# A hybrid decoder block on one core: ScalarE alone reads the turned banks of q and k, and the zero column of a weight tile is set by the engine that takes its differences

## The chip, the core and the metric

The kernel runs on one core of a Trainium2 chip. A core has TensorE (PE; its weight loads are listed apart as PEld), VectorE (DVE), ScalarE (ACT), GpSimd (POOL) and SyncE (SP), which issues transfers. Each engine takes its own instructions in the order in which they were written to its queue, and waits for the others through semaphores. The metric is the device time of one execution in microseconds (us), the median over runs; lower is better.

## The reference, cut to what matters

One decoder layer over 1024 tokens of width 1024, all in float32: a projection of the normalized input into three groups of heads (a short convolution, attention, a gated MLP), an output projection, a squared-ReLU MLP of width 4096 and a gated embedding. The change lies in the attention group, and there in two places: the normalized q and k, and the step from `log_rem` to `weights`.

```
q = rms_norm(q.reshape(bsz, s_len, 8, 64), q_norm_g)
k = rms_norm(k.reshape(bsz, s_len, 8, 64), k_norm_g)
...
z = einsum('bqhd,bkhd->bhqk', q, k) * 64 ** -0.5        # blocks of 128 queries
causal = s_pos < t_pos
log_beta = log_sigmoid(z)
log_rem = where(causal, log_sigmoid(-z), 0.0)
suffix = cumsum(log_rem, axis=3, reverse=True) - log_rem
weights = where(causal, exp(log_beta + suffix), 0.0)
o = einsum('bhqk,bkhd->bqhd', weights, v)
```

## The kernel before, in words

A float32 operand of a product is kept as two tiles, a `hi` part in the type fp32r and a `lo` part, the rest (`src - hi`). A product is then three matmuls, hi by hi, hi by lo and lo by hi (`product`, L157; `run`, L808). ScalarE makes the hi parts and VectorE, mostly, the lo parts (`split`, L131).

The program has four stages by the profile's clock: a first one to about 85 us (gating MLP, first projection), attention to about 395 us, the rest of the convolution and the output projection, and from about 480 us on the MLP and the gate. The change lies in the first two.

`project(pr)` (L345) makes q, k and v for a pair of heads. For each of eight blocks of 128 tokens, 24 matmuls write `qkv_ps`; the mean square of each head goes ScalarE (`qk_sq`, L376), VectorE (`ss`, L379), GpSimd (`rs`, L170), and VectorE scales q and k with it into the tile `qk` (L384). ScalarE and VectorE then write the two parts of `V` (L391).

Two blocks later, so to speak, `turn_qk` (L395) handles a pair of blocks: TensorE transposes four 128x128 squares of `qk` into one PSUM bank, `qk_tr`, q on its left half and k on its right. ScalarE writes the hi part of q (`QS`, L137 through `split`), VectorE its lo part (`q_lo`, L138), ScalarE the hi part of k (`KH`, L407), and VectorE its lo part in two halves of 64 partitions (`KL`, L409). All five read the bank. After the last block of a half (t = 3 and 7), six copies (L413 to L418) rearrange the parts. `qk_tr` comes from the pool `ps_tr` of three banks, in which the attention's own transposes `w_tr` take their turn too.

`attend(pr)` (L423) works on the same pair of heads. `stick(hh, g)` makes two rows of 128 queries (t = 2g and 2g+1) of head hh: matmuls `z` (L448, L450), a sigmoid on ScalarE into `rem` (L452), a scan on VectorE (L457; its backward running product is the exponential of the suffix sums), and the differences of neighbours into the weight tile `wt` (L464), on VectorE for t = 3, 5, 7 and on GpSimd for the others. The last column of `wt` is set to zero by GpSimd before that (L463). `wt` has four buffers. `gather(hh, g)` transposes the weight tiles into `w_tr` (L486), splits them (`wT_hi` on ScalarE, `wT_lo` on VectorE) and multiplies with `V` (`av`, L504). Head 0 goes through g = 0 to 3, head 1 through g = 3 to 0, so the wide rows of head 1 follow on those of head 0.

While pair `pr` is attended to, the projection of the next pair (for the last pair, the convolution) is woven in as fill for TensorE (`weave`, L269). The order in which the code is emitted isn't the order on the engines: the program is scheduled as a whole (`schedule_with_timeline_sim`, L1341), so that a changed instruction can move its neighbours on all engines.

Of the kernel before, what the change touches and what calls it, by code (L numbers as in the profile page):

```python
# [10 lines left out]
AF = mybir.ActivationFunctionType  # L11
ALU = mybir.AluOpType
# [21 lines left out]
def hybrid_block(ctx: ExitStack, tc: tile.TileContext, a: dict):  # L34
# [5 lines left out]
    nc = tc.nc  # L40
# [84 lines left out]
    gq = load_const("gq", [P, 1])  # L125
# [5 lines left out]
    def split(src, hi, lo, scale=None, low=nc.vector):  # L131

        if scale is None:
            last_hi[0] = nc.scalar.copy(hi, src)  # L134
            low.tensor_tensor(out=lo, in0=src, in1=hi, op=ALU.subtract)  # L135
        else:
            nc.scalar.activation(hi, src, AF.Copy, scale=scale)  # L137
            nc.vector.scalar_tensor_tensor(out=lo, in0=src, scalar=scale, in1=hi,  # L138
                                           op0=ALU.mult, op1=ALU.subtract)
# [255 lines left out]
    def turn_qk(head, t, qk):  # L395

        QS, KH, KL, _, low_q = head
        th = t // 4
        tr = bank(ps_tr, "qk_tr")
        for i in range(2):  # L400
            for j in range(2):
                o = j * 256 + i * P
                nc.tensor.transpose(tr[:, o:o + P], qk[:, i, j * P:(j + 1) * P], ident)
        ws = slice((t % 4 - 1) * P, (t % 4 + 1) * P)

        split(tr[:, :256], QS[0][th][:, ws], low_q[th][:, ws], scale=gq)
        nc.scalar.activation(KH[0][th][:, ws], tr[:, 256:], AF.Copy, scale=gk)  # L407
        for hh, own in enumerate((lo_p, hi_p)):
            nc.vector.scalar_tensor_tensor(out=KL[hh][th][own, ws], in0=tr[own, 256:],  # L409
                                           scalar=gk[own], in1=KH[0][th][own, ws],  # L410
                                           op0=ALU.mult, op1=ALU.subtract)
        if t % 4 == 3:
            nc.scalar.copy(KH[1][th][hi_p], KH[0][th][hi_p])  # L413
            nc.scalar.copy(KH[1][th][lo_p], KH[0][th][hi_p])
            nc.scalar.copy(KH[0][th][hi_p], KH[0][th][lo_p])
            nc.vector.tensor_copy(QS[1][th][hi_p], QS[0][th][hi_p])
            nc.vector.tensor_copy(QS[1][th][lo_p], low_q[th][hi_p])
            nc.vector.tensor_copy(QS[0][th][hi_p], low_q[th][lo_p])  # L418
        return 8
# [3 lines left out]
    def attend(pr):  # L423

        QS, KH, KL, V, _ = heads[pr]
# [11 lines left out]
        def stick(hh, g):  # L437
            weights[hh, g] = []
            for t in (2 * g, 2 * g + 1):
                W = (t + 1) * P  # L440
                th, ts = block(t)
                rem = at.tile([P, T], F32, tag="rem", name=name("rem"), bufs=3)
                wt = at.tile([P, T], F32, tag="wt", name=name("wt"), bufs=4)
                for kh in reversed(range(th + 1)):
                    n = min(HT, W - kh * HT)
                    ks = slice(kh * HT, kh * HT + n)
                    z = bank(ps_z, "z")[:, :n]
                    nc.tensor.matmul(z, QS[hh][th][:, ts], KH[hh][kh][:, :n],  # L448
                                     start=True, stop=False)
                    nc.tensor.matmul(z, QS[hh][th][:, ts], KL[hh][kh][:, :n],  # L450
                                     start=False, stop=True)
                    last_act[0] = nc.scalar.activation(rem[:, ks], z, AF.Sigmoid,  # L452
                                                       scale=-HD ** -0.5)


                back = rem[:, :W][:, ::-1]
                nc.vector.tensor_tensor_scan(out=back, data0=back,  # L457
                                             data1=after[:, T - W:][:, ::-1], initial=1.0,
                                             op0=ALU.mult, op1=ALU.max)


                on_vector = t in (3, 5, 7)
                nc.gpsimd.memset(wt[:, W - 1:W], 0.0)  # L463
                done = (nc.vector if on_vector else nc.gpsimd).tensor_tensor(  # L464
                    out=wt[:, :W - 1], in0=rem[:, 1:W], in1=rem[:, :W - 1], op=ALU.subtract)
                if not on_vector:
                    last_pool[0] = done
                weights[hh, g].append(wt)
                yield 2 * (t + 1) + 8
# [455 lines left out]
    for h in range(2):  # L925
        for n in (0, 4, 1, 5, 2, 6, 3, 7):
# [28 lines left out]
            t = hg[n][h] = late_slot("tmp", "hg")  # L955
# [29 lines left out]
    for i in range(FT):  # L985
# [19 lines left out]
        if i == 0:  # L1005
# [6 lines left out]
            for p, bank in last_k:  # L1012
                done = run(bank, up_pairs.pop((0, p)), hn[p], False, True, slice(3, 4))
# [27 lines left out]
        done = product_up(bc, 4, False, True)  # L1041
# [98 lines left out]
    for s, (c, p, j) in enumerate(steps):  # L1140
# [13 lines left out]
        elif p == 6:  # L1154
            subtract(nc.vector, u_sum[j], u_sum[j], bank)
            if last:
                add(nc.vector, h_res[j][1], h_res[j][1], u_sum[j])
                for h in range(2):
                    t = residual(j + 4, h)
                    subtract(nc.vector, t, t, u_sum[j])  # L1160
        elif p in (2, 3):
            t = residual(j, p - 2)
# [3 lines left out]
        else:  # L1166
            h = 0 if p == 4 else 1
            t = residual(j + 4, h)
# [55 lines left out]
    for p in GATE:  # L1224
        for j in range(4):
# [14 lines left out]
            for bank, c in zip(banks, cs):  # L1240
                done = run(bank, w, [cols(b, c) for b in h3[p]], p not in MATE, p not in (1, 7))
# [7 lines left out]
                elif p == 5:  # L1249
                    e_of[j] = late_slot("tmp", "e")  # L1250
                    add(nc.vector, e_of[j], bank, v_of[j])
                    t = late_slot("tmp", "gt")
                    add(nc.vector, t, d_bank.pop((3, j))[0], e_of[j])
                    gated(j, 1, t, t, c, by_dma=True)
                elif p == 7:
                    t = e_of[j][:, c]
                    add(nc.vector, t, bank, t)
                    gated(j + 4, 1, t, t, c, -1.0, True)
                elif p == 4:
                    t = v_of[j][:, c]  # L1260
# [84 lines left out]
```

## Time and profile before

| | us |
|---|---|
| median of 3 runs | 1207.3 (1204.84 to 1210.0) |
| the profiled execution | 1206.75 |
| its span, first to last instruction | 1205.0 |
| busy: PE | 1181.0 (98%) |
| busy: DVE | 885.7 (73%) |
| busy: ACT | 595.5 (49%) |
| busy: POOL | 400.5 (33%) |

The span is the time between the first and the last instruction of the profiled execution; 1.75 us of its time lie around it. A row such as `q_lo<-qk_tr,c_gq,QS x16 | 7.5, 471 | 0.6` names the tile written and those read, the count, the busy time in us with the mean of one in ns, and the idle time of the engine just before these instructions. A wait is put down to the engine that ended it. Matmuls overlap each other in the records, so that a busy TensorE isn't TensorE at its peak; its idle time is where it had nothing it could start.

### The profile page before, as it was taken

The numbers are of one execution on the slowest core, as the hardware profiler recorded it, in microseconds if no ns is written. First come the engines' busy times: TensorE is split into PE (matmuls) and PEld (weight loads), VectorE is DVE, ScalarE is ACT, GpSimd is POOL, SyncE is SP. The second block draws the span as 40 slices with busy tenths as digits, with TensorE's granted clock in tenths as the row PEclk, the third lists the DMA queues.
The fourth block names the chain that finished last, engine by engine and source line by source line (L and its number), as shares of the span: only waits on it lengthen the run. The fifth ranks groups of instructions, "written<-read, shape, count | busy, mean of one in ns | idle before, by whom it ended". The sixth has DMA issues, their size and how long they took to land.

```text
span 1205.0 us, 17538 instructions
## 1 busy us (share of the span) xinstructions
PE 1181.0 (98%) x5788; PEld 1007.1 (84%) x5788; DVE 885.7 (73%) x1310; ACT 595.5 (49%) x1148; POOL 400.5 (33%) x472
## 2 busy tenths in 40 slices
PE   9999899998999999999999999999999999999997
PEld 7899899898888888888888888888888888888886
DVE  7846898989896667868877777787664657753697
ACT  7735565565643466733334333356543444456642
POOL 3324355464352222045354453421023301013412
PEclk9999999999999999999999999999999999999999
DMA  9602359999673776679998989777889975644857
GB/s 311 233 18 90 130 172 262 253 194 167 140 146 95 196 263 204 204 207 261 265 240 249 264 238 260 221 257 277 300 267 295 290 249 175 231 146 119 181 155 209
DMA packets 127963, 254.03 MB, mean 211 GB/s; under 512 B 14496, under 2 KB 22432, under 8 KB 127168
## 3 DMA queue, kind: packets, MB, share of 16 engines
q1 hardware_dynamic: 94992, 168.08, 41.4%
q0 software_dynamic: 27664, 57.05, 25.2%
q10 hardware_dynamic: 5216, 27.79, 6.4%
q8 instruction: 45, 0.74, 0.3%
q14 instruction: 46, 0.38, 0.1%
HBM read 192.30 MB, written 92.80 MB: 237 GB/s over the span
## 4 chain that ended last, share of the span: by engine, by line
PE 88%; DVE 8%; ACT 1%; issue 1%; DMA 1%; POOL 1%; SPq 0%; DVEq 0%; ACTq 0%; POOLq 0%
PE f_ps L814 25%; PE d_ps L814 25%; PE g_ps L814 6%; DVE rem L457 3%; PE qkv_ps L161 3%; PE qkv_ps L162 2%; PE qkv_ps L163 2%; PE o_ps L161 2%; PE o_ps L163 2%; PE o_ps L162 2%; PE av L504 2%; PE cv_ps L163 2%; PE cv_ps L161 2%; PE cv_ps L162 2%; PE w_tr L486 1%; PE vu_ps L162 1%
## 5 line engine op out<-in xcount | busy, mean ns | idle before, releaser
L135 DVE TENSOR_TENSOR w_lo<-raw,w_hi 128x512 fp32r<-128x512 f32 x280 | 243.1, 872 | 85.0 <-ACT w_hi L134 83.1
L134 ACT CAST w_hi<-raw 128x512 fp32r<-128x512 f32 x280 | 172.5, 620 | 240.5 <-PE d_ps L814 115.4
L814 PE MATMUL f_ps<-hn_hi,w_hi 128*128 128x512 f32 x448 | 175.2, 392 | 0.0
L814 PE MATMUL f_ps<-hn_lo,w_hi 128*128 128x512 f32 x448 | 174.9, 390 | 0.0
L814 PE MATMUL d_ps<-f_hi,w_hi 128*128 128x512 f32 x448 | 174.8, 390 | 0.0
L814 PE MATMUL f_ps<-hn_hi,w_lo 128*128 128x512 f32 x448 | 174.6, 391 | 0.0
L814 PE MATMUL d_ps<-f_hi,w_lo 128*128 128x512 f32 x448 | 174.3, 389 | 0.0
L814 PE MATMUL d_ps<-f_lo,w_hi 128*128 128x512 f32 x448 | 174.3, 389 | 0.0
L457 DVE TENSOR_TENSOR_SCAN rem<-rem,after 128x128 f32<-128x128 f32 (+3 forms) x64 | 90.9, 1431 | 13.3 <-ACT rem L452 13.3
L814 PEld LDWEIGHTS f_ps<-hn_lo,w_hi 128*128 128x128 f32 x448 | 84.5, 189 | 17.9 <-issue 0.2
L814 PEld LDWEIGHTS f_ps<-hn_hi,w_hi 128*128 128x128 f32 x448 | 84.5, 189 | 17.8 <-issue 0.2
L814 PEld LDWEIGHTS f_ps<-hn_hi,w_lo 128*128 128x128 f32 x448 | 84.5, 189 | 17.6
L814 PEld LDWEIGHTS d_ps<-f_hi,w_hi 128*128 128x128 f32 x448 | 84.1, 188 | 17.7 <-issue 0.2
L814 PEld LDWEIGHTS d_ps<-f_hi,w_lo 128*128 128x128 f32 x448 | 84.1, 188 | 17.6
L814 PEld LDWEIGHTS d_ps<-f_lo,w_hi 128*128 128x128 f32 x448 | 84.1, 188 | 17.5 <-issue 0.2
L161 PE MATMUL qkv_ps<-whi,xn_hi 128*128 128x384 f32 x256 | 88.8, 347 | 0.9 <-DVE V L138 0.8
L162 PE MATMUL qkv_ps<-wlo,xn_hi 128*128 128x384 f32 x256 | 86.6, 338 | 0.0
L163 PE MATMUL qkv_ps<-whi,xn_lo 128*128 128x384 f32 x256 | 86.3, 337 | 0.0
L135 DVE TENSOR_TENSOR f_lo<-raw,f_hi 128x512 fp32r<-128x512 f32 x112 | 78.2, 728 | 8.5 <-ACT f_hi L134 8.2
L134 ACT CAST f_hi<-raw 128x512 fp32r<-128x512 f32 x112 | 67.1, 620 | 25.6 <-DMA raw<-f_dram 21.6
L800 POOL TENSOR_TENSOR S<-S,sq 128x512 f32<-128x512 f32 x19 | 25.6, 1347 | 160.1 <-ACT sq L876 160.1
L452 ACT ACTIVATE rem<-z 128x128 f32<-128x128 f32 (+3 forms) x96 | 46.7, 500 | 24.3 <-PE z L450 21.6
(250 smaller groups left out, 2618.9 us busy)
## 6 DMA issues: line engine op xcount, KB each, us to landing
raw<-in_w_ff SPq DMA_DIRECT2D x148, 256.0 KB, 4.2
raw<-f_dram SPq DMA_DIRECT2D x112, 256.0 KB, 5.1
raw<-w_sums SPq DMA_DIRECT2D x64, 256.0 KB, 4.1
f_dram<-f SPq DMA_DIRECT2D x48, 256.0 KB, 3.9
f_dram<-t SPq DMA_DIRECT2D x48, 256.0 KB, 4.0
w_sums<-in_w_ff POOLq DMA_DIRECT2D x8, 1024.0 KB, 12.1
w_sums<-w_sums POOLq DMA_DIRECT2D x8, 1024.0 KB, 15.3
raw<-in_w_out SPq DMA_DIRECT2D x28, 256.0 KB, 3.5
```

The costliest lines, as they stand in the source:

```text
L134: last_hi[0] = nc.scalar.copy(hi, src)
L135: low.tensor_tensor(out=lo, in0=src, in1=hi, op=ALU.subtract)
L161: nc.tensor.matmul(ps, lh, rh, start=first and i == 0, stop=False)
L162: nc.tensor.matmul(ps, lh, rl, start=False, stop=False)
L163: done = nc.tensor.matmul(ps, ll, rh, start=False, stop=last and i == len(terms) - 1)
L452: last_act[0] = nc.scalar.activation(rem[:, ks], z, AF.Sigmoid, scale=-HD ** -0.5)
L457: nc.vector.tensor_tensor_scan(out=back, data0=back, data1=after[:, T - W:][:, ::-1], initial=1.0, op0=ALU.mult, op1=ALU.max)
L486: nc.tensor.transpose(tr[:, n:n + P], wts[i][:, kb * P:(kb + 1) * P], ident)
L504: nc.tensor.matmul(av[:, first * P:], lhs, part[:, o:o + m], start=kb == 0 and part is hi, stop=kb == 2 * g + 1 and part is lo)
L800: return eng.tensor_tensor(out=out, in0=x, in1=y, op=ALU.add)
L814: done = nc.tensor.matmul(bank, l, r, start=first and k == 0 and i == 0, stop=k == len(b) - 1 and i == 2, skip_group_check=True)
```

## The change

In `turn_qk`, ScalarE writes the hi parts of q and k and then copies the whole bank into the `qk` tile from which it was transposed. VectorE takes its three lo parts (`q_lo`, two `KL`) from that copy in SBUF, no longer from the bank. In `stick`, the zero column is set by VectorE where VectorE takes the differences (t = 3, 5, 7: 24 of the 64 tiles), and by GpSimd for the other 40.

```diff
-        split(tr[:, :256], QS[0][th][:, ws], low_q[th][:, ws], scale=gq)
+        nc.scalar.activation(QS[0][th][:, ws], tr[:, :256], AF.Copy, scale=gq)
         nc.scalar.activation(KH[0][th][:, ws], tr[:, 256:], AF.Copy, scale=gk)
+        turned = qk.rearrange("p t c -> p (t c)")
+        nc.scalar.copy(turned, tr)
+        nc.vector.scalar_tensor_tensor(out=low_q[th][:, ws], in0=turned[:, :256], scalar=gq,
+                                       in1=QS[0][th][:, ws], op0=ALU.mult, op1=ALU.subtract)
         for hh, own in enumerate((lo_p, hi_p)):
-            nc.vector.scalar_tensor_tensor(out=KL[hh][th][own, ws], in0=tr[own, 256:],
+            nc.vector.scalar_tensor_tensor(out=KL[hh][th][own, ws], in0=turned[own, 256:],
                                            scalar=gk[own], in1=KH[0][th][own, ws],
                                            op0=ALU.mult, op1=ALU.subtract)
...
                 on_vector = t in (3, 5, 7)
-                nc.gpsimd.memset(wt[:, W - 1:W], 0.0)
-                done = (nc.vector if on_vector else nc.gpsimd).tensor_tensor(
+                eng = nc.vector if on_vector else nc.gpsimd
+                eng.memset(wt[:, W - 1:W], 0.0)
+                done = eng.tensor_tensor(
                     out=wt[:, :W - 1], in0=rem[:, 1:W], in1=rem[:, :W - 1], op=ALU.subtract)
```

Counted over the program: ScalarE gets 16 copies more, VectorE 24 memsets more, GpSimd 24 fewer. No transfer and no matmul is added or removed, but the scheduler places the instructions of the attention stage anew on every engine; from the end of that stage on, the order is the same row for row.

ScalarE, in the first wide rows of head 1 while the second pair of heads is attended to. Before, the two hi parts of one bank (`QS_2262`, `KH_2261`, both from `qk_tr_2534`) have other work between them:

```order
L137 ACTIVATE QS_2262<-qk_tr_2534,c_gq 128x256
L452 ACTIVATE rem_2569<-z_2571 128x384
L452 ACTIVATE rem_2569<-z_2575 128x512
L375 COPY qk_sq_2949<-ms_729 128x4
L407 ACTIVATE KH_2261<-qk_tr_2534,c_gk 128x256
L137 ACTIVATE V_2557<-qkv_ps_2460,r_569 128x2x64
```

The same place now:

```order
L407 ACTIVATE QS_2269<-qk_tr_2542,c_gq 128x256
L408 ACTIVATE KH_2268<-qk_tr_2542,c_gk 128x256
L410 COPY qk_2372<-qk_tr_2542 128x512
L457 ACTIVATE rem_2578<-z_2580 128x384
L457 ACTIVATE rem_2578<-z_2584 128x512
L137 ACTIVATE V_2566<-qkv_ps_2468,r_569 128x2x64
```

The two hi parts and the copy stand together, ahead of the two sigmoids that used to come between them.

VectorE at the same place before: the lo part of q, the differences of t = 7 (`wt`, 1023 columns), the scan of t = 6 (896 columns), then the lo parts of k:

```order
L379 TENSOR_REDUCE ss_2644<-qk_sq_2641 128x4
L138 SCALAR_TENSOR_TENSOR q_lo_2263<-qk_tr_2534,c_gq,QS_2262 128x256
L464 TENSOR_TENSOR wt_2468<-rem_2467 128x1023
L457 SCALAR_TENSOR_TENSOR rem_2569<-rem_2569,after 128x896
L409 SCALAR_TENSOR_TENSOR KL_2257<-qk_tr_2534,c_gk,KH_2261 64x256
L409 SCALAR_TENSOR_TENSOR KL_2259<-qk_tr_2534,c_gk,KH_2261 64x256
L384 TENSOR_TENSOR qk_2555<-qkv_ps_2560,rs_2646 128x256
L138 SCALAR_TENSOR_TENSOR V_2557<-qkv_ps_2460,r_569,V_2557 128x2x64
L457 SCALAR_TENSOR_TENSOR rem_2588<-rem_2588,after 128x1024
```

VectorE there now:

```order
L379 TENSOR_REDUCE ss_2653<-qk_sq_2650 128x4
L470 TENSOR_TENSOR wt_2476<-rem_2475 128x1023
L411 SCALAR_TENSOR_TENSOR q_lo_2270<-qk_2372,c_gq,QS_2269 128x256
L414 SCALAR_TENSOR_TENSOR KL_2264<-qk_2372,c_gk,KH_2268 64x256
L414 SCALAR_TENSOR_TENSOR KL_2266<-qk_2372,c_gk,KH_2268 64x256
L462 SCALAR_TENSOR_TENSOR rem_2578<-rem_2578,after 128x896
L138 SCALAR_TENSOR_TENSOR V_2566<-qkv_ps_2468,r_569,V_2566 128x2x64
L384 TENSOR_TENSOR qk_2564<-qkv_ps_2569,rs_2655 128x256
L462 SCALAR_TENSOR_TENSOR rem_2597<-rem_2597,after 128x1024
```

The differences have moved ahead of the lo part of q, and all three lo parts stand ahead of the scan of 896 columns; what lies between the two scans of 1024 columns is the same nine instructions.

A little later on VectorE, where the memset comes in. Before:

```order
L464 TENSOR_TENSOR wt_2589<-rem_2588 128x1023
L379 TENSOR_REDUCE ss_2768<-qk_sq_2765 128x4
L457 SCALAR_TENSOR_TENSOR rem_2725<-rem_2725,after 128x768
L464 TENSOR_TENSOR wt_2726<-rem_2725 128x767
L135 TENSOR_TENSOR wT_lo_2676<-w_tr_2671,wT_hi_2675 128x384
```

And now:

```order
L470 TENSOR_TENSOR wt_2598<-rem_2597 128x1023
L379 TENSOR_REDUCE ss_2778<-qk_sq_2775 128x4
L462 SCALAR_TENSOR_TENSOR rem_2734<-rem_2734,after 128x768
L469 MEMSET wt_2735 128x1
L135 TENSOR_TENSOR wT_lo_2685<-w_tr_2680,wT_hi_2684 128x384
L470 TENSOR_TENSOR wt_2735<-rem_2734 128x767
```

The memset of a tile stands one instruction ahead of its differences, with a lo part of transposed weights between them.

## Rows read from the trace of the kernel before

**Rows 1.** The profile's page: busy time of each engine with its share of the span, the busy tenths of TensorE and VectorE in 40 slices of 30 us, and the chain of work that ended last, by engine.

```profile
PE 1181.0 (98%) x5788; PEld 1007.1 (84%) x5788; DVE 885.7 (73%) x1310; ACT 595.5 (49%) x1148; POOL 400.5 (33%) x472
...
PE   9999899998999999999999999999999999999997
...
DVE  7846898989896667868877777787664657753697
...
PE 88%; DVE 8%; ACT 1%; issue 1%; DMA 1%; POOL 1%; SPq 0%; DVEq 0%; ACTq 0%; POOLq 0%
```

**Rows 2.** Busy time by stretches of the span: length, then the busy us (and instructions) of PE, PEld, DVE, ACT and POOL, the granted TensorE clock, the DMA share and GB/s. First the attention stage as a whole, then the three stretches in which the wide rows of head 1 are worked on beside a projection, then the stage after 480 us.

```profile
85.00:395.00 310.00, 296.68 (x1824) 272.81 (x1823) 259.67 (x395) 166.68 (x401) 146.62 (x199) 1.00 0.66 163
...
142.00:167.00 25.00, 22.04 (x142) 19.95 (x141) 24.45 (x33) 14.33 (x35) 8.90 (x15) 1.00 0.23 85
...
207.00:233.00 26.00, 23.46 (x149) 21.10 (x149) 25.37 (x34) 15.48 (x37) 13.50 (x15) 1.00 0.99 235
...
273.00:299.00 26.00, 22.64 (x145) 20.17 (x144) 24.78 (x32) 14.71 (x36) 12.92 (x16) 1.00 0.96 175
...
480.00:1205.00 725.00, 716.63 (x3197) 593.29 (x3195) 508.27 (x709) 328.86 (x563) 206.16 (x213) 0.99 0.78 232
```

**Rows 3.** Waits of TensorE in the attention stage: who waited for whom, us in total, times, the longest.

```profile
PE w_tr L486 <- DVE KL L409: 3.6, 4, 1.5
PE w_tr L486 <- DVE wt L464: 3.2, 3, 1.6
PE av L504 <- DVE wT_lo L135: 2.9, 4, 1.8
PE qk_tr L403 <- DVE qk L384: 1.5, 1, 1.5
PE qkv_ps L161 <- DVE V L138: 0.8, 2, 0.5
PE av L504 <- DVE y_b L522: 0.5, 1, 0.5
PE w_tr L486 <- DVE wT_lo L135: 0.3, 1, 0.3
```

**Rows 4.** Instructions in order of time around one of these waits (start us, us, engine, line, what, and the idle time before it): VectorE, and TensorE's transposes that waited, there and at two more of the four places.

```profile
211.80 0.47 DVE L138 SCALAR_TENSOR_TENSOR q_lo<-qk_tr,c_gq,QS 128x256 fp32r<-128x256 f32 x1
212.20 1.21 DVE L464 TENSOR_TENSOR wt<-rem 128x1023 f32<-128x1023 f32 x1
213.33 2.01 DVE L457 TENSOR_TENSOR_SCAN rem<-rem,after 128x896 f32<-128x896 f32 x1
215.26 0.96 DVE L409 SCALAR_TENSOR_TENSOR KL<-qk_tr,c_gk,KH 64x256 fp32r<-64x256 f32 x2
...
216.36 0.63 PE L486 MATMUL w_tr<-ident,wt 128*128 128x128 f32 x4 [0.86 <-DVE KL L409]
...
149.93 0.30 PE L486 MATMUL w_tr<-ident,wt 128*128 128x128 f32 x1 [0.94 <-DVE KL L409]
...
282.77 0.63 PE L486 MATMUL w_tr<-ident,wt 128*128 128x128 f32 x4 [1.54 <-DVE KL L409]
```

**Rows 5.** Groups of instructions of the attention stage by shape: count, busy us and mean ns of one, idle us before them and what ended it.

```profile
L409 DVE SCALAR_TENSOR_TENSOR KL<-qk_tr,c_gk,KH 64x256 fp32r<-64x256 f32 x32 | 15.3, 479 | 1.5 <-ACT KH L407 1.1
...
L138 DVE SCALAR_TENSOR_TENSOR q_lo<-qk_tr,c_gq,QS 128x256 fp32r<-128x256 f32 x16 | 7.5, 471 | 0.6 <-ACT QS L137 0.5
...
L659 DVE SCALAR_TENSOR_TENSOR cv_acc<-cv_u,c_conv_w,cv_acc 128x1 f32<-128x1 f32 x1 | 0.2, 210 | 0.0
...
L407 ACT ACTIVATE KH<-qk_tr,c_gk 128x256 fp32r<-128x256 f32 x16 | 7.6, 476 | 9.1 <-DVE q_lo L138 9.0
...
L590 ACT COPY y_c<-c_tr 128x512 f32<-128x512 f32 x2 | 1.2, 586 | 0.4 <-PE c_tr L588 0.4
```

**Rows 6.** The zero columns on GpSimd over the whole span (ns: shortest, median, longest), and what GpSimd waited for in the attention stage.

```profile
L463 POOL MEMSET wt<- x64: 88/100/1360, 74.4 to 380.5; 128x1 f32 x64
...
POOL wt L463 <- PE w_tr L486: 40.7, 13, 6.6
```

**Rows 7.** VectorE instructions with both inputs in SBUF: the lo parts of the projection's weights, as a group of the attention stage and three of them in order of time, with what ran on GpSimd at the time.

```profile
L135 DVE TENSOR_TENSOR wlo<-stage,whi 128x384 fp32r<-128x384 f32 x23 | 20.6, 905 | 0.6 <-PE cv_ps L163 0.6
...
112.84 0.55 DVE L135 TENSOR_TENSOR wlo<-stage,whi 128x384 fp32r<-128x384 f32 x1
...
114.59 2.35 DVE L135 TENSOR_TENSOR wlo<-stage,whi 128x384 fp32r<-128x384 f32 x2
...
112.94 4.87 POOL L135 TENSOR_TENSOR wlo<-stage,whi 128x384 fp32r<-128x384 f32 x4
```

**Rows 8.** The differences of the weight tiles on VectorE in the attention stage, by shape, both inputs in SBUF, and their shortest, median and longest over all shapes.

```profile
L464 DVE TENSOR_TENSOR wt<-rem 128x1023 f32<-128x1023 f32 x8 | 10.5, 1312 | 0.0
...
L464 DVE TENSOR_TENSOR wt<-rem 128x511 f32<-128x511 f32 x8 | 7.9, 985 | 1.0 <-PE w_tr L486 0.8
L464 DVE TENSOR_TENSOR wt<-rem 128x767 f32<-128x767 f32 x8 | 7.6, 951 | 0.2
...
L464 DVE TENSOR_TENSOR wt<-rem x24: 675/1044/2028, 119.8 to 378.0; 128x511 f32<-128x511 f32 x8, 128x767 f32<-128x767 f32 x8, 128x1023 f32<-128x1023 f32 x8
```

## The prediction

> **What bounds the kernel now.** Begin with the page [rows 1]: TensorE is busy 98% of the span, so all that can be won without taking work from it is 24 us (1205.0 less 1181.0), and the change takes none. The chain of waits puts 88% on TensorE and 8%, some 96 us, on VectorE; the slices show where VectorE reaches 8 and 9 tenths, between 120 and 360 us. So go on to the stretches [rows 2]. After 480 us the engines' order doesn't change, and that stage stays. The attention stage, 85 to 395 us, holds 13.3 us of TensorE's idle time (310 less 296.68), and 8.9 us of it fall into three stretches of 77 us in all (2.96, 2.54 and 3.36), those in which the wide rows of head 1 run beside a projection. There VectorE has 0.55, 0.63 and 1.22 us of idle time, 2.4 together, in place of TensorE's 8.9. In these stretches VectorE sets the pace, and TensorE, whose queue holds a fixed share of fill, waits for it; elsewhere in the stage VectorE has 47.9 us to spare (50.3 less 2.4). An addition to VectorE is therefore paid in full in the three stretches and hidden outside of them. That is the rule by which I price everything below.
>
> Last, the waits themselves [rows 3]. The longest sum, 3.6 us in four waits, is what the change aims at: transposes `w_tr` that wait for the lo parts of k. They don't need `KL`; they need the bank that `qk_tr` holds until `KL` has read it. The order of time shows why it is held long [rows 4]: behind the lo part of q come the differences (1.21 us) and a scan (2.01 us) before VectorE gets to `KL`, and TensorE is idle 0.86 us until then.
>
> **The bank is given back by ScalarE.** ScalarE now reads the bank three times in a row, and `KL` no longer holds it. The four waits of 3.6 us go. But what is late next? The waits fall into the stretches where VectorE is hardly ever idle (at 149.9, 216.4 and 282.8 us by [rows 4]; 3.3 of the 3.6 us). If TensorE transposes earlier there, ScalarE's copy of the transposed weights is early too, and then lies waiting for VectorE, which has the same instructions between the same two scans as before, in another order. TensorE's wait then moves to the next `wT_lo` or `wt` [rows 3]. What can be gained is bounded by 3.6 us above and by nothing below, if VectorE's total alone decides. As VectorE's own idle time in the stretches is 2.4 us, and part of it can close when ScalarE is ahead, I take half: -1.8 us (0 to -3.6).
>
> **The copies.** There are 16 on ScalarE, priced by the copy of a 128x512 bank, 586 ns [rows 5]: 9.4 us. Against them stand 9.0 us that ScalarE spent waiting in front of `KH` for `q_lo` [rows 5], because the two took turns at the bank; that turn is gone. ScalarE has 143 us idle in the stage (310 less 166.68), and some 32 of the 77 us in the three stretches [rows 2]. I count 0. With that cover gone, the six copies in the stretches would cost 3.5 us.
>
> **A longer wait for the lo parts.** `q_lo` now waits for the copy, thus for `KH` and the copy beyond the hi part of q: 476 and 586 ns [rows 5], 1.06 us. Queued behind it on VectorE are the two `KL`, a scan and the lo parts of the weights, for which TensorE waits. Today `q_lo` waited 0.5 us for ScalarE in all 16 cases [rows 5]: VectorE comes to it late, and in the wide stretches it has the differences of 1.21 us ahead of it now. So 0; if VectorE stood there each time, six times 1.06 or 6.4 us in the stretches.
>
> **The lo parts read SBUF on both sides.** By themselves they last as long as before, about 471 and 479 ns [rows 5], since no row shows a gain from the source. But with both inputs in SBUF they can meet GpSimd. The weights' lo parts of this kind last 0.55 us when GpSimd starts one just after [rows 7]; two of them beside GpSimd's four take 2.35 us, and their mean in the stage is 905 ns, 0.355 us more than 0.55. The differences of 1023 columns, which stand next to `q_lo` in the very stretches, last 1.21 us at best [rows 4] and 1.312 in the mean [rows 8], 0.10 us more; those of 511 columns 675 ns at best and 985 in the mean [rows 8], 0.31 more. Two of a projection's four turned banks fall into each stretch, six in all, so 18 lo parts: from 0 to 18 x 0.355 = 6.4 us. The nearest row is that of the same place, 0.10: +1.8 us. The other 30 are hidden in the 47.9 us.
>
> **The memsets.** 24 go to VectorE, three in each stretch (t = 7, 5 and 3): nine that count. VectorE has no memset in these rows. Its smallest instruction of one column takes 210 ns [rows 5], GpSimd's memset 88 at best and 100 in the middle [rows 6]: 9 x 0.088 = 0.8 to 9 x 0.21 = 1.9 us. I take 0.15 each, +1.4 us. GpSimd loses 24 of 64 memsets, in front of which it waited 40.7 us for transposes [rows 6]; it has time to spare, 163 us in the stage [rows 2], and I count nothing for it.
>
> **The rest of the order** is shuffled within some microseconds, and I put 0 on that, with 1.8 us either way, the longest single wait that TensorE has for a `wT_lo` [rows 3].
>
> **The sum.** -1.8 + 0 + 0 + 1.8 + 1.4 = +1.4 us. Against the profiled execution, 1206.75, that is 1208.15; this execution lies 0.55 us below the median of 1207.3, which I leave out of account. I predict 1208 us, no difference that can be told: a measurement of this kernel can tell some 0.5% or 6 us from none, so below 1201.3 counts as faster and above 1213.3 as slower. The likeliest case's own range, from the ends of its terms, is 1202 to 1213.
>
> **Rivals.**
> *Order, not total, sets TensorE's wait.* If TensorE's idle time in the stretches comes from what stands ahead of what, rather than from VectorE's sum, then the freed bank (3.6 us) and the differences that now stand ahead of `q_lo` and not behind it (they end 3.2 us of waits [rows 3]) give both sums: 1206.75 - 6.8 = 1200 us; all 13.3 us gone would give 1193.5. For it: TensorE's waits are few and long, and the two lines are the longest of the list. Against it: VectorE is idle 2.4 us in 77. Chance 0.25.
>
> *The lo parts collide with GpSimd.* In the three stretches each of the 18 waits as the weights' lo parts do, 0.355 us, the bank's gain is eaten by a VectorE that is later still, and the memsets cost 1.9: 1206.75 + 6.4 + 1.9 = 1215 us. It decides from 0.26 us for each ((6.55 - 1.9) / 18), where 1213.3 is passed. For it: GpSimd is busy half of the stretches (35.3 of 77 us, rows 2), with differences and powers that read SBUF. Against it: the row of the same place says 0.10. Chance 0.13. The Trainium skill has a rule that speaks for this rival ("SBUF — State Buffer", section "Who interferes with whom"): a VectorE instruction with two SBUF inputs takes its second through a read interface that it shares with GpSimd, and whichever holds it first makes the other wait to its end, while one with a single SBUF input is never in the way. By that rule the old lo parts, with one side in PSUM, were safe and the new ones are not; 2.35 us for two that take 0.55 alone [rows 7] agrees with it.
>
> *The memset blocks VectorE.* It waits until the transposes of four tiles earlier have freed the buffer. On GpSimd that took 40.7 us in 13 waits, 3.1 each [rows 6]; three such waits among the nine in the stretches are 9.4 us, or 1216 us. Against it: the differences behind it need the same buffer anyway. Chance 0.07.
>
> **How the numbers follow.** My forecast of no difference gets 0.55, the first rival 0.25, the two on the slow side 0.20 together. A range for 8 times in 10 leaves out about a tenth at each end: 1198 on the fast side, just below the first rival, and 1216, the slow rivals' own times.
>
> **What would show it.** The profile after should have no wait of `w_tr` for `KL`, and none of `KH` for `q_lo`. If VectorE's total decides, TensorE's waits for `wT_lo` and `wt` grow as those for `KL` go, and VectorE is still idle under 3 us in the three stretches. `q_lo` and `KL` by their mean show the collisions: 0.57 us for my term, 0.73 or more for the rival. The memsets' mean and the wait before them show the last two terms. I am wrong if TensorE's idle time in the stage falls below some 7 us, or rises above 19.

## The result, and the profile after

Over 8 timed runs each, the changed kernel takes 1212.5 us (1210.78 to 1214.51) and the one before 1207.7: a ratio of 1.0036, 95% interval 1.0023 to 1.0049. By that ratio it is slower by 4.4 us, a third of a per cent. That stays within the half per cent that I had said a measurement can't tell from none; with this many runs it can be told.

The page of the changed kernel, its profiled execution of 1210.78 us:

```profile
span 1209.1 us, 17547 instructions
...
PE 1181.1 (98%) x5788; PEld 1006.1 (83%) x5788; DVE 895.8 (74%) x1334; ACT 599.8 (50%) x1164; POOL 396.2 (33%) x448
```

TensorE's work is the same (1181.0 us before, [rows 1]); 4 us of idle time were added. Of these, 1.05 us lie in the first 30 us, in TensorE's waits for the hi parts of the first weights, which change from trace to trace (1.3 us before, 2.3 now, 2.9 in the fastest kernel of the experiments), and 2.6 us in the attention stage. VectorE is busy 10.1 us longer, but only 3.2 us of that lie in the stage (262.90 against 259.67 [rows 2]); most of the rest comes after 480 us, where the order is the same. By windows (length, busy us of PE, PEld, DVE, ACT, POOL, granted clock):

```profile
85.00:395.00 310.00, 294.06 (x1799) 269.45 (x1799) 262.90 (x416) 171.52 (x415) 141.13 (x173) 1.00 0.65 159
```

Within the stage, the same window of the clock doesn't hold the same work in both kernels. The changed one starts the first scan of 1024 columns of a pair of heads 0.7, 2.2, 3.5 and 2.6 us later than the kernel before (first to fourth pair). So the stage is cut here at these scans, one piece for each pair, the last one ending with the last transpose. The kernel before:

```profile
142.84:209.28 66.44, 62.01 (x404) 58.63 (x403) 60.57 (x89) 38.74 (x97) 33.94 (x47) 1.00 0.66 196
209.28:274.90 65.62, 63.01 (x412) 59.55 (x410) 58.82 (x89) 39.31 (x98) 38.08 (x53) 1.00 0.94 212
274.90:341.33 66.43, 62.47 (x376) 54.77 (x375) 60.27 (x93) 38.48 (x90) 28.37 (x44) 1.00 0.76 154
341.33:391.43 50.10, 50.01 (x279) 42.40 (x278) 40.19 (x51) 19.29 (x40) 20.93 (x26) 1.00 0.52 116
```

The changed kernel:

```profile
143.53:211.53 68.00, 62.72 (x406) 59.12 (x405) 60.87 (x95) 39.81 (x101) 33.56 (x42) 1.00 0.66 191
211.53:278.43 66.90, 63.45 (x410) 59.52 (x408) 60.31 (x96) 40.57 (x103) 38.56 (x47) 1.00 0.92 209
278.43:343.95 65.52, 62.11 (x369) 54.01 (x368) 59.72 (x97) 39.63 (x94) 26.46 (x37) 1.00 0.77 153
343.95:396.72 52.77, 51.27 (x284) 43.27 (x283) 43.06 (x54) 19.31 (x40) 18.62 (x23) 1.00 0.51 114
```

TensorE is idle 4.43, 2.61, 3.96 and 0.09 us in the four pieces before, and 5.28, 3.45, 3.41 and 1.50 after. The largest addition, 1.4 us, stands in the last pair's rows, which run beside the convolution: VectorE has 9.7 us to spare there, and no copy and no lo part of q or k is left (the last `KL` starts at 330.1 us). The three stretches of [rows 2], each moved by the delay of its pair, are:

```profile
142.69:167.69 25.00, 20.70 (x132) 18.48 (x131) 24.08 (x31) 13.91 (x33) 6.33 (x10) 1.00 0.23 85
209.25:235.25 26.00, 23.12 (x145) 20.31 (x145) 25.61 (x36) 16.39 (x39) 14.05 (x13) 1.00 0.98 232
276.53:302.53 26.00, 22.86 (x141) 19.75 (x140) 25.12 (x35) 16.08 (x39) 12.56 (x14) 1.00 0.97 174
```

In them TensorE is idle 10.3 us (4.30, 2.88 and 3.14), against 8.9 before; VectorE 2.2 us, against 2.4. (Windows that are not moved show 8.1 us for TensorE, as if it had gained.)

The last transpose of the stage starts at 391.4 us before and 396.7 after. TensorE's longest waits in the stage, after:

```profile
PE qkv_ps L161 <- DVE V L138: 6.5, 6, 1.8
PE av L510 <- DVE wT_lo L135: 3.5, 6, 0.9
PE w_tr L492 <- DVE wt L470: 1.9, 3, 0.9
```

The wait of `w_tr` for `KL` (3.6 us, [rows 3]) is gone, and so are ScalarE's 9.0 us in front of `KH` [rows 5]. In its place stands one that had cost 0.8: the next projection's matmuls wait for the bank that VectorE's part of `V` reads last. The transposes were freed and TensorE ran into the next thing VectorE owes it.

VectorE's own groups (count, busy us, mean ns | idle time before them), first the scans of 1024 columns before (L457), then the changed kernel's:

```profile
L457 DVE TENSOR_TENSOR_SCAN rem<-rem,after 128x1024 f32<-128x1024 f32 x8 | 19.2, 2403 | 1.7 <-ACT rem L452 1.7
...
L462 DVE TENSOR_TENSOR_SCAN rem<-rem,after 128x1024 f32<-128x1024 f32 x8 | 22.9, 2867 | 0.4 <-ACT rem L457 0.4
L414 DVE SCALAR_TENSOR_TENSOR KL<-qk,c_gk,KH 64x256 fp32r<-64x256 f32 x32 | 17.1, 534 | 0.2
L411 DVE SCALAR_TENSOR_TENSOR q_lo<-qk,c_gq,QS 128x256 fp32r<-128x256 f32 x16 | 8.7, 543 | 2.5 <-ACT qk L410 2.1
L469 DVE MEMSET wt<- 128x1 f32 x24 | 1.4, 59 | 2.3 <-PE w_tr L492 2.2
```

The lo parts are 55 and 72 ns longer in the mean than in [rows 5], and the scans of 1024 columns, which the change doesn't touch, grew from 2403 to 2867 ns. The order of time, VectorE and then GpSimd (POOL), shows how:

```profile
148.60 2.03 DVE L462 TENSOR_TENSOR_SCAN rem<-rem,after 128x896 f32<-128x896 f32 x1
150.54 0.59 DVE L138 SCALAR_TENSOR_TENSOR V<-qkv_ps,r,V 128x128 fp32r<-128x128 f32 x2
151.04 3.56 DVE L462 TENSOR_TENSOR_SCAN rem<-rem,after 128x1024 f32<-128x1024 f32 x1
...
150.77 1.68 POOL L470 TENSOR_TENSOR wt<-rem 128x895 f32<-128x895 f32 x1 [5.75 <-DVE rem L462]
```

When the scan of 896 columns ends, GpSimd starts its differences (1.68 us), and the next scan, which lasts 2.29 us when no differences run beside it (at 143.53 us), takes 3.56. Before, the two `KL` stood between these scans and read the bank. After, both stand ahead of the scan of 896, and the scan of 1024 comes upon GpSimd. The Trainium skill's rule that I set beside my second rival ("SBUF — State Buffer", "Who interferes with whom") says so of two SBUF inputs, and that who issues first decides who waits. (For one input it excepts VectorE's two-port modes, which my sentence left out.) The scan agrees with it: it ends 2.15 us after GpSimd's differences do, about the 2.29 us that it takes alone.

### The profile page after: what moved, and what is told of

The parts are those of the page before. It is cut to its first block, busy times and chain, and to the rows that moved or that the text cites. A ratio compares the mean times of both kernels' runs of the same rounds, so it can differ in the third digit from the quotient of the medians.

```text
span 1209.1 us, 17547 instructions
## 1 busy us (share of the span) xinstructions
PE 1181.1 (98%) x5788; PEld 1006.1 (83%) x5788; DVE 895.8 (74%) x1334; ACT 599.8 (50%) x1164; POOL 396.2 (33%) x448
## 4 chain that ended last, share of the span: by engine, by line
PE 85%; DVE 9%; issue 2%; DMA 1%; ACT 1%; POOL 0%; ACTq 0%; SPq 0%; DVEq 0%; POOLq 0%
PE f_ps L820 25%; PE d_ps L820 25%; PE g_ps L820 4%; PE qkv_ps L161 3%; DVE rem L462 3%; PE qkv_ps L163 3%; PE qkv_ps L162 3%; PE o_ps L163 2%; PE o_ps L161 2%; PE o_ps L162 2%; PE av L510 2%; PE cv_ps L161 1%; PE cv_ps L162 1%; PE cv_ps L163 1%; PE w_tr L492 1%
## 5 line engine op out<-in xcount | busy, mean ns | idle before, releaser
L135 DVE TENSOR_TENSOR w_lo<-raw,w_hi 128x512 fp32r<-128x512 f32 x280 | 247.3, 888 | 87.8 <-ACT w_hi L134 84.1
L462 DVE TENSOR_TENSOR_SCAN rem<-rem,after 128x128 f32<-128x128 f32 (+3 forms) x64 | 93.1, 1471 | 11.2 <-ACT rem L457 11.0
L170 POOL TENSOR_TENSOR rs<-ss,mhalf 128x4 f32<-128x4 f32 x32 | 40.3, 1259 | 62.1 <-DVE ss L379 54.8
```

What stands on the lines that cost most here:

```text
L170: last_power[0] = nc.gpsimd.tensor_tensor(out=out, in0=in_, in1=mhalf[:, :n], op=ALU.pow)
L462: nc.vector.tensor_tensor_scan(out=back, data0=back, data1=after[:, T - W:][:, ::-1], initial=1.0, op0=ALU.mult, op1=ALU.max)
```

## The experiments

Each is timed in five rounds beside the kernel before on the same chip; ratios are to that kernel. The letters: S, the scans beside GpSimd's differences cost the time; L, the lo parts themselves, reading SBUF; M, the memsets on VectorE; C, ScalarE's copies; D, lo parts that start later; X, copy and source together; O, the order.

**The copies alone.** The memsets stay on GpSimd:

```diff
-                eng.memset(wt[:, W - 1:W], 0.0)
+                nc.gpsimd.memset(wt[:, W - 1:W], 0.0)
```

> Only the first half of the change: ScalarE's copy of the turned bank, lo parts from the copy; all zero columns stay on GpSimd. Theory S (the scans of 1024 columns now follow so closely on those of 896 that they meet GpSimd's 895-wide differences and wait for them; seen in the changed kernel as a mean of 2867 ns against 2403): the copy moved the lo parts, so the scans' mean stays at 2.8 us or more and the time is 3 to 5 us above before, 1211 to 1213. Theory L (the lo parts themselves wait for GpSimd, 543 and 534 ns against 471 and 479): the same time, with the same means. Theory M (the memsets on VectorE cost it): back to within 1 us of before, about 1208.

1213.2 us, 1.0042 (1.0029 to 1.0054): all of the loss, without the memsets, and in nearly the changed kernel's order.

**The memsets alone.** The kernel before with the second hunk of the diff.

> Only the second half: 24 zero columns set by VectorE, the bank read by both engines as before. Theory S and L: within 1 us of before (24 x 59 ns = 1.4 us of VectorE, the scans' mean at 2.4 us, lo parts at 471 and 479 ns), about 1208. Theory M: 3 us or more above before, 1211 or more.

1209.1 us, 1.0002 (0.9993 to 1.0011). They cost nothing, and M falls.

**`KL` behind the scan again.** In the changed kernel, the two `KL` of a projection's first turned bank (t = 1; the expectations of two later runs call it the second) are held back while a pair is attended to, and queued behind the scan of 896 columns, where they stood before:

```diff
+        if t == 1 and attended[0]:
+            held.append(k_low)
...
+                if hh == 1 and t == 6:
+                    with tc.issue_after(scan.ins):
+                        while held:
+                            held.pop(0)()
```

> The changed kernel with one thing moved: for the first turned bank of each of the three later pairs, the two lo parts of k stand behind the scan of 896 columns instead of ahead of it (as they stood before the change), still reading the copy in SBUF. Theory S: the 0.97 us of lo parts between the two scans let GpSimd finish, the scans of 1024 columns return to a mean of about 2.45 us (three of them 1 us shorter each), and the time falls by about 3 us to 1209 to 1210. Theory L: the lo parts read what they read in the changed kernel, so the time stays at 1212 to 1213. Theory M: the same 1212 to 1213.

1215.5 us, 1.0057 (1.0045 to 1.0070). The scans are back at 2341 ns, and the kernel is slower still. Now the `KL` are what comes upon GpSimd; their mean is 682 ns. In order of time, VectorE and then GpSimd:

```profile
220.25 2.27 DVE L416 SCALAR_TENSOR_TENSOR KL<-qk,c_gk,KH 64x256 fp32r<-64x256 f32 x2
222.56 0.35 DVE L138 SCALAR_TENSOR_TENSOR V<-qkv_ps,r,V 128x128 fp32r<-128x128 f32 x1
...
220.48 1.76 POOL L481 TENSOR_TENSOR wt<-rem 128x895 f32<-128x895 f32 x1 [0.42 <-DVE rem L468]
```

Two take 2.27 us, where 0.96 was usual [rows 4], and `V` stands behind them: TensorE's wait for `V` sums to 8.5 us. The scans aren't needed for a loss; here another collision stands in their place.

**Adjacent hi parts, no copy.** The changed kernel, but the lo parts read the bank:

```diff
-        turned = qk.rearrange("p t c -> p (t c)")
-        nc.scalar.copy(turned, tr)
+        turned = tr
```

> The changed kernel without the copy: ScalarE writes the hi parts of q and k one after the other, and VectorE then takes all lo parts from the bank. Theory S: the lo parts still stand ahead of the scan of 896 columns in two of the three places, so the scans' mean stays at 2.7 us or more and the time at 1211 to 1213; the waits of the transposes for the lo parts of k come back. Theory L: lo parts back at 471 and 479 ns, time back to about 1209. Theory M: 1212 to 1213.

1208.2 us, 0.9992 (0.9981 to 1.0003), although the scans of 1024 columns take 2785 ns. So there is an order in which these collisions cost nothing, and S falls as a sufficient cause. What costs hangs on the copy, or on the order that is made around it.

**The copy made and not read.** As the last, with the copy left in:

```diff
-        turned = qk.rearrange("p t c -> p (t c)")
-        nc.scalar.copy(turned, tr)
+        nc.scalar.copy(qk.rearrange("p t c -> p (t c)"), tr)
+        turned = tr
```

> Edit: the changed kernel with its 16 copies on ScalarE, but the lo parts of q and k read the bank as before; nobody reads the copy. Theory L (the lo parts, once both their inputs lie in SBUF, lose to GpSimd, and the V and weights behind them are late): 1208.5 us, KL and q_lo means at 479 and 471 ns, TensorE's wait for V near 1 us. Theory C (the copies take ScalarE's time in the stretches where it also copies turned weights): 1211.5 us or more, as much as the changed kernel, with ScalarE busy 9.6 us more than in the run without a copy.

1211.1 us, 1.0031 (1.0017 to 1.0045). Nothing reads SBUF that didn't before, and most of the loss is there: L isn't needed for it.

**The same, copy first and the hi part of q last.**

> Edit: as the run with the idle copy, but ScalarE makes the copy first and the hi part of q last, so that the lo part of q waits for all three of ScalarE's instructions, as in the changed kernel, and still reads the bank. Theory L: 1208.5 us. Theory D (what costs time is that the lo parts are later by the copy, 0.6 us each in 16 turned banks, not what they read): 1211.5 us or more, with waits of q_lo for ScalarE of 2 us or more.

1209.6 us, 1.0014 (1.0006 to 1.0023). The lo part of q has to wait longest here, and the kernel is faster than the last: no sign of D. But the two stand in different orders, and a price of the wait could hide behind that.

**The changed kernel with the copy first.** ScalarE: copy, hi part of k, hi part of q.

> Edit: the changed kernel with ScalarE's copy first, then the hi part of k, then that of q; the lo parts read the copy. The bank is held as long as in the changed kernel; KL can start one ScalarE instruction earlier. Theory L: 1212 us as the changed kernel, KL and q_lo means of 520 ns or more. Theory D: 1210 us, since KL no longer waits for the last of the three. Theory C: 1212 us.

1211.0 us, 1.0018 (1.0008 to 1.0028), about half the loss. Between this and the last the edit changes the source alone, and the ratios differ by 0.0004; between the changed kernel and the idle copy by 0.0005. Both are within the error. But in each of these pairs hundreds of TensorE's rows stand in another order too, so the price of the source by itself isn't measured.

**No copy, `KL` behind the scan, memsets on GpSimd.** Of the change only the adjacent hi parts are left, plus the edit that puts `KL` back.

> Edit: no copy; the two hi parts stand next to each other on ScalarE, the lo parts read the bank, the KL of the second turned bank stand behind the scan of 896 columns as in the kernel before, all zero columns are set by GpSimd. So the only thing left of the change is that ScalarE no longer waits between the hi parts. Theory L: no cost left, 1207 us, scans of 1024 columns at 2.4 us. If the order of VectorE (scans of 1024 columns beside GpSimd's differences, 2.79 us in the run with adjacent hi parts) is worth something, up to 4 x 0.4 = 1.6 us less than that run, 1206.5 us; otherwise 1208.2 us.

1206.0 us, 0.9975 (0.9965 to 0.9985): faster than both kernels, and half a microsecond below the least that was expected.

**This with the idle copy.**

> Edit: the kernel of e8 (hi parts adjacent, lo parts read the bank, KL of the second turned bank behind the scan of 896 columns, all zero columns set by GpSimd) with the 16 copies on ScalarE added behind the two hi parts; nobody reads the copy. Theory C (ScalarE's copy costs the time, wherever the lo parts read): 1211 us, 4 to 5 us above e8, as e5 (with the idle copy) stood above e4 (without it). Theory L: 1206 us as e8, KL mean 479 ns. Theory X (copy and source cost only together with an order in which a KL meets GpSimd's differences): 1206 to 1208 us here and above 1213 us in e10.

1213.2 us, 1.0031 (1.0018 to 1.0044): 16 copies that nobody reads cost 0.0056, some 6.8 us, some 70% of all the time they take (16 at 597 ns), on an engine that is idle half of the time. C's number, but hard to believe as a price of 16 copies.

**This with the lo parts reading the copy.**

> Edit: the kernel of e9, but the lo parts read the copy in SBUF, so that source alone differs from e9. Theory L or X: 5 us or more above e9, 1213 us or more, KL mean about 680 ns as in e3 (which is this kernel with 24 of the zero columns set by VectorE), TensorE's waits for V above 6 us and its granted clock falling after them as in e3. Theory C: within 2 us of e9.

1215.3 us, 1.0051 (1.0034 to 1.0068). `KL` are at 641 ns and TensorE's waits for `V` at 7.9 us; with the order that was made around it, the source costs 0.0020, by intervals that meet. L and X had asked for 0.004.

**The idle copy in a fixed order.** When an instruction is added, the scheduler lays the whole program out anew: between the kernels with and without the idle copy, hundreds of rows differ on TensorE. So I fixed the order. The instructions of each engine were numbered as traced, and every one is made to stand behind the one that it follows in the kernel without the copy; only the copies are free, each behind its `KH`.

```diff
+            tc.add_manual_dep(nxt, one.name, mybir.DependencyInfo(
+                mybir.DependencyClass.NoSync, mybir.DependencyReason.DATA), reason="pin")
```

> Edit: the kernel of e9 (idle copy of each turned bank on ScalarE, lo parts reading the bank), but every engine's instructions are fixed in the order that e8 (without the copy) has, and each copy stands on ScalarE directly behind the hi part of k. So it differs from e8 by 16 instructions of about 0.6 us on ScalarE and nothing else, and from e9 by the order alone, which the scheduler had made anew around the copies. Theory C (the copies take time of ScalarE that the path needs): 1.003 of the kernel before, as e9, 6 us above e8. Theory O (the copies cost next to nothing; what costs is the other order that the program is given when they are in it): 0.998, within 1.5 us of e8, with TensorE's idle time in the stage near e8's 11.2 us and not e9's 15.8 us.

1207.2 us, 0.9991 (0.9982 to 1.0001). The copies by themselves cost 0.0016 (0.9991 less 0.9975), 1.9 us; the order made around them 0.0040 (1.0031 less 0.9991), 4.8 us. The instructions are the same in both, and the intervals lie apart: O is shown for this pair. TensorE is idle 15.8 us in the attention stage in the scheduler's order, and 11.3 in the fixed one (11.2 in the kernel without copies):

```profile
85.00:395.00 310.00, 294.19 (x1800) 270.93 (x1799) 259.52 (x392) 172.32 (x415) 143.13 (x197) 0.99 0.66 159
...
85.00:395.00 310.00, 298.68 (x1828) 275.44 (x1827) 255.57 (x394) 172.69 (x417) 146.96 (x199) 0.99 0.67 162
```

The longest wait shows how. In the scheduler's order (VectorE, then TensorE, then a window of the clock):

```profile
187.72 1.13 DVE L481 TENSOR_TENSOR wt<-rem 128x511 f32<-128x511 f32 x1
188.77 0.41 DVE L385 TENSOR_TENSOR qk<-qkv_ps,rs 128x256 f32<-128x256 f32 x1
...
189.24 0.44 PE L404 MATMUL qk_tr<-ident,qk 128*128 128x128 f32 x2 [2.71 <-DVE qk L385]
...
192.00:196.00 4.00, 4.00 (x22) 4.00 (x21) 2.61 (x6) 1.83 (x4) 0.00 (x0) 0.74 0.58 121
```

In the fixed order:

```profile
187.90 0.40 DVE L385 TENSOR_TENSOR qk<-qkv_ps,rs 128x256 f32<-128x256 f32 x1
188.21 0.94 DVE L482 TENSOR_TENSOR wt<-rem 128x511 f32<-128x511 f32 x1
...
188.35 0.44 PE L404 MATMUL qk_tr<-ident,qk 128*128 128x128 f32 x2 [0.73 <-DVE qk L385]
```

Two neighbours on VectorE have changed places, the differences now standing ahead of the scaling of q and k. TensorE, which has another order of fill as well, waits 2.71 us for it instead of 0.73, and its granted clock is down behind that wait (0.83 from 188 to 192 us and 0.74 in the four after, where the fixed order has 1.00).

The copies' own 1.9 us don't show as time that ScalarE lacked, since TensorE's idle time is that of the kernel without them. TensorE's one long wait for ScalarE in the fixed order comes behind another copy, `y_both`, that waited 3.79 us for a transfer (ScalarE, then TensorE, then the clock):

```profile
281.26 0.37 ACT L531 COPY y_both<-av 128x256 f32<-128x256 f32 x1 [3.79 <-DMA y_dram<-y_both]
...
282.19 0.50 PE L460 MATMUL z<-KH,QS 128*128 128x512 f32 x1 [2.99 <-ACT rem L464]
...
284.00:288.00 4.00, 4.00 (x15) 3.81 (x16) 4.00 (x6) 1.38 (x4) 4.00 (x3) 0.64 1.05 188
```

Whether that belongs to the copies, one trace can't tell.

**The changed kernel's order without the copy.** The same device the other way: the operations of the run with adjacent hi parts, in the order of the changed kernel.

> Edit: the changed kernel without its 16 copies, the lo parts of q and k reading the bank, and every engine's instructions fixed in the order that the changed kernel has. So it differs from the changed kernel by the copy and by what the lo parts read, and from the run with adjacent hi parts (e4) by the order alone. Theory O (the order that the scheduler made around the copies costs the time): 1.002 or more of the kernel before, 1210 us and up; with the copy's own price as e11 gave it, 0.0016, 1.0036 less that is 1.002. Theory C+L (copy and source cost it, the order nothing): 0.9992 to 1.000 as e4, 1208 us.

1212.1 us, 1.0028 (1.0016 to 1.0040). The number is O's, but it isn't clean:

```profile
PE w_tr L491 <- DVE KL L413: 10.5, 6, 3.6
```

The changed kernel's order puts transposes early, counting on a bank that the copy gives back; without the copy they wait 10.5 us for `KL`. So in its own order the copy does earn something, and this run prices an order with what it was made for taken out. Against the run with adjacent hi parts, whose instructions are the same, the order alone makes 0.0036, by intervals that lie apart (1.0028 against 0.9992). How much of the changed kernel's 4.4 us is order isn't settled by that.

One part is settled. In the last pair's rows, cut as above, this run, with no copy, has the changed kernel's idle time (52.77 us less 51.28, or 1.49, against 1.50):

```profile
345.32:398.09 52.77, 51.28 (x285) 43.27 (x284) 43.05 (x54) 19.30 (x40) 18.68 (x23) 1.00 0.51 115
```

The run of the copies alone, whose memsets stay on GpSimd, has 1.49 there too. The kernel before has 0.09, the run with adjacent hi parts 0.10. So these 1.4 us come neither from the copy nor from the source nor from the memsets: they are the order.

## Why the prediction was right

I had forecast 1208 us, no difference within 0.5%, and a sum of +1.4; measured are +4.4 and 1212.5, inside the range of 1198 to 1216. TensorE's idle time in the stage, 15.9 us, lies between the 7 and 19 that I had set as signs of being wrong. The class was right, with 4.4 of its 6 us used up. It held by its width, not by the sum, whose terms came out otherwise: that is luck in part. Part of the size, 1.4 us at the least, came from a term that I had put at zero. (The likeliest case's range up to 1213 doesn't follow from its terms: their upper ends, 0 + 3.5 + 6.4 + 6.4 + 1.9 + 1.8, add up to +20. 1213 is the bound of the class.)

*The bank, -1.8.* The four waits went, and the wait moved on to VectorE's next result, as the working said. I named `wT_lo` and `wt`, which went from 2.9 to 3.5 and from 3.2 to 1.9 us; it was `V`, which had 0.8 us in [rows 3] and has 6.5 now. Nothing was gained: TensorE's idle time in the stretches rose by 1.5 us.

*The copies, 0 (to 3.5).* At a fixed order 0.0016, 1.9 us, with the intervals of the two runs just meeting; the trace doesn't show where.

*The longer wait for the lo parts, 0.* `q_lo` waited 2.1 us for the copy over 16 cases, and where it has to wait for all three of ScalarE's instructions (1.0014), the kernel was faster than where it needn't (1.0031). That fits 0, but the order differed too.

*The lo parts in SBUF, +1.8.* The term was for the three stretches, and there it is next to nothing: `KL` takes 478 to 479 ns in the mean (474 to 481 before) and `q_lo` 477 to 482 (464 to 470 before). Over the program they lengthened VectorE by 16 x 0.072 + 32 x 0.055 = 2.9 us, most of it at one place outside of the stretches, beside GpSimd's lo parts of weights (VectorE, GpSimd, and TensorE's wait behind them, in the changed kernel; last, VectorE's `V` there before):

```profile
114.30 1.24 DVE L411 SCALAR_TENSOR_TENSOR q_lo<-qk,c_gq,QS 128x256 fp32r<-128x256 f32 x1
115.46 2.36 DVE L414 SCALAR_TENSOR_TENSOR KL<-qk,c_gk,KH 64x256 fp32r<-64x256 f32 x2
117.85 0.35 DVE L138 SCALAR_TENSOR_TENSOR V<-qkv_ps,r,V 128x128 fp32r<-128x128 f32 x1
118.12 1.02 DVE L135 TENSOR_TENSOR wlo<-stage,whi 128x384 fp32r<-128x384 f32 x2
...
113.80 2.61 POOL L135 TENSOR_TENSOR wlo<-stage,whi 128x384 fp32r<-128x384 f32 x2
...
118.26 0.44 PE L161 MATMUL qkv_ps<-whi,xn_hi 128*128 128x384 f32 x1 [1.83 <-DVE V L138]
...
114.32 0.35 DVE L138 SCALAR_TENSOR_TENSOR V<-qkv_ps,r,V 128x128 fp32r<-128x128 f32 x1
```

The three take 2.15 us more than their usual 0.48 and 0.97, and `V` comes behind them. GpSimd had cost VectorE time there before as well, on the weights' lo parts: 2.35 us for two [rows 7], which now take 1.02. But `V` stood ahead of those. So the collision grew by 0.9 us, and moved ahead of `V`; what it costs depends on who stands behind it. In the whole kernel's time, pairs of runs that differ in the source, and in the order with it, lie 0.0004, 0.0005 and 0.0020 apart. That the term came near 2.9 us is luck.

What I missed is the scans: 8 x 0.464 = 3.7 us of VectorE, and 2.7 of it in the stretches, where VectorE is full (3.56, 3.48 and 3.48 us, against 2.52, 2.46 and 2.81 before). Of the collision I asked only which instructions change their source, not which ones change their neighbours. What this cost isn't shown: the run with adjacent hi parts has long scans too, and lost nothing, in an order of its own.

*The memsets, +1.4.* 59 ns each, under the lower of my bounds, and nothing in the time. (VectorE's nine differences in the stretches are two of t = 7 and one of t = 5 in each, none of t = 3.)

*The order, 0 ± 1.8.* This is the step that failed, by its size. "The rest of the order is shuffled within some microseconds" took for its bound the longest single wait. With instructions held equal, two orders differ by 4.8 us, and two others by 0.0036, some 4.4 us. In the changed kernel itself, 1.4 us of TensorE's idle time in the last pair's rows are order and nothing else; how much of the other 3 us is, stays open. The rule by which I priced everything stood by half. In the three stretches VectorE is still full (2.2 us idle), and TensorE waits for it. That the rest of the stage hides additions holds only for the order that it was read from: in the last pair's rows TensorE is now idle 1.50 us, with VectorE free for 9.7 us of 52.8.

The first rival said that order and not total sets TensorE's waits. The rule was right, as far as the fixed orders show; its forecast, that the freed bank would therefore gain 6.8 us, was wrong, since it let the order change only for the better. The second rival asked for 0.26 us on each lo part; they took 0.06. The third fell with the run of the memsets alone; in the changed kernel VectorE waited 2.2 us for transposes in front of its memsets, over the whole stage, where the rival had 9.4.

## What to carry to other kernels

In a program that a scheduler lays out as a whole, an edit's price has two parts: what its instructions cost, and what the new layout costs. Where the two could be told apart here, the second was the larger (4.8 against 1.9 us), so bound it by the spread between layouts of the same work and not by one wait. To tell the two apart, fix each engine's order and add the instruction to it; experiments that let the order float answer another question. And when two traces are compared by windows, cut them at the same instruction and not at the same microsecond: a kernel that is 2 us late shows its waits in the next window.

Before a VectorE operand is moved from PSUM to SBUF, list what GpSimd runs beside it, and beside those instructions that then stand in its former place. The best kernel here has no copy: hi parts adjacent, lo parts from the bank, `KL` behind the scan, 0.9975. Whether its 3 us come from the adjacent hi parts or from its order wasn't separated.

## What the runs showed of the hardware

TensorE's granted clock fell behind some of its longer idle times, and stayed up behind others as long. Windows of the last run (the changed kernel's order without the copy), with idle times of 3.62 us ending at 148.2 and 3.01 ending at 216.0:

```profile
144.00:148.00 4.00, 0.58 (x5) 0.39 (x3) 3.97 (x6) 1.59 (x5) 0.51 (x1) 1.00 0.00 0
148.00:152.00 4.00, 3.80 (x15) 3.07 (x16) 3.94 (x5) 2.16 (x5) 1.68 (x1) 0.58 0.00 0
...
212.00:216.00 4.00, 1.02 (x8) 0.74 (x6) 3.95 (x7) 1.77 (x6) 3.20 (x4) 1.00 0.93 138
216.00:220.00 4.00, 3.97 (x17) 3.59 (x18) 3.97 (x4) 2.05 (x5) 2.51 (x4) 0.61 1.12 219
```

The windows behind the gaps show 0.58 and 0.61: most of them at 1.2 GHz rather than 2.4. By estimate from that share, each loses some 1.6 us (0.4 of 4 us) on top of the wait. The changed kernel's wait of 1.83 us before 118.3 was followed by a full clock:

```profile
116.00:120.00 4.00, 2.17 (x14) 1.93 (x13) 3.95 (x9) 1.56 (x5) 1.99 (x4) 1.00 0.25 71
120.00:124.00 4.00, 4.00 (x28) 3.96 (x27) 2.89 (x8) 2.34 (x7) 1.68 (x3) 1.00 0.84 257
```

and one of 1.78 us before 123.4 in the run of the memsets alone was not:

```profile
124.00:128.00 4.00, 4.00 (x19) 4.00 (x18) 3.66 (x11) 3.81 (x11) 2.10 (x4) 0.58 0.83 247
```

So a wait that an order makes longer can cost more than its own length. The run with `KL` behind the scan in the changed kernel had three such falls in the wide stretches, behind waits for `V` (0.78, 0.74 and 0.71 in the windows after them, the last one shown), and by this trace part of its 1.0057 is theirs:

```profile
292.00:296.00 4.00, 4.00 (x19) 4.00 (x18) 4.00 (x5) 0.00 (x0) 0.00 (x0) 0.71 1.12 206
```
